# Adding the products of a GpSimd convolution in two instructions of 256 columns instead of one of 512

## The chip, the cores and the metric

The kernel runs on one core of a Trainium2 chip. The metric is the device time of one execution in microseconds (us). TensorE multiplies matrices, VectorE, ScalarE and GpSimd work elementwise, and SyncE issues the transfers from memory; in rows of the profile they are PE (PEld for its weight loads), DVE, ACT, POOL and SP.

## What is computed

Two transformer blocks on 512 tokens of 1024 channels. The change is in the first layer of the second block, layer A, whose mixer is this:

```python
def conformer_conv(u, conv_w, conv_b, g, b):
    a, gl = jnp.split(u, 2, axis=-1)
    h = a * jax.nn.sigmoid(gl)
    h = jnp.pad(h, ((0, 0), (CONV_KERNEL - 1, 0), (0, 0)))
    h = lax.conv_general_dilated(h, conv_w[:, None, :].astype(h.dtype), (1,), 'VALID',
                                 dimension_numbers=('NWC', 'WIO', 'NWC'),
                                 feature_group_count=CONV_WIDTH_2) + conv_b
    return jax.nn.silu(layer_norm(h, g, b))
```

That is a convolution along the tokens, channel by channel, with 31 taps on 1536 channels, and then a layer norm over the channels. Beside it the layer computes attention to a memory of 256 rows, a gate, and an output projection.

## The kernel before

Activations lie with channels on the 128 partitions and the 512 tokens along the columns, so 1536 channels are 12 tiles of 128x512. Matrix products are exact to float32 by splitting: each weight tile is loaded to `raw`, ScalarE copies it to `whi` (the high part) and VectorE computes `wlo` = `raw` - `whi` (the low part, `prep`, L445 to L455), and TensorE makes three products of the parts (`mm3`, L457). A product can't start before its `wlo` is there. I call the instruction at L453 a split. There are 3 buffers for `raw`, and 4 each for `whi` and `wlo`.

`conv_tile(j)` (L1134 to L1162) makes one of the 12 tiles of the convolution. Two projections give the gate and the value; VectorE writes their product to `pad`, which has 30 leading columns set to 0 by GpSimd. The 31 taps are shared out over the engines (`NOFF, NPE = 11, 1`, L591):
- tap 0: ScalarE writes the sum `cg`.
- taps 1 to 10: ScalarE multiplies a shifted view of `pad` by the tap's weight into `tm`, and GpSimd adds `tm` to `cg` in one instruction of 128x512 (L1149 to L1152). That is 10 adds to a tile and 120 in all.
- tap 11: TensorE, by a diagonal matrix, into a PSUM bank `cp`.
- taps 12 to 30: VectorE adds them to `cp`, 19 instructions to a tile (L1160), 228 in all. They read one operand from SBUF and one from PSUM.

VectorE then adds `cp` to `cg` (L1161), and the layer norm `lnc` (L1132, class `LN`) takes the tile: GpSimd subtracts a mean from it and adds up its squares. Gate tiles, attention and part of the output projection are woven between the 12 tiles (`weave`, L1011 and L1203).

No engine runs in this order of the text. The class `Program` records every instruction (L137), and `order` (L233) makes a plan from estimated durations: at each moment every free engine takes the ready instruction with the best priority. `emit` (L359) repeats that 12 times with new priorities, keeps the plan with the earliest end, and issues the instructions in its order. Each engine then runs its own list strictly in that order. Three properties of the plan matter here:
- It follows dependencies by whole tiles (L148 to L156), so two writes to different columns of one tile depend on each other. Between dependent GpSimd instructions it puts 102 ns (L52).
- It treats instructions marked `port` as exclusive, over VectorE and GpSimd together. Every GpSimd instruction over more than 8 columns is marked (L188), and on VectorE those with two wide operands from SBUF, such as the split (L186). VectorE's taps are not.
- A marked instruction whose port is taken at the moment when its engine is free is passed over, and the engine takes the next ready one:

```python
                    if o.port and port > now:
                        heapq.heappush(events, port)
                        continue
```

It charges a GpSimd instruction with two operands `n * 2.2 + 99` ns for n columns (L188).

Of the kernel before, what the change touches and what calls it, by code (L numbers as in the profile page):

```python
# [13 lines left out]
ALU = mybir.AluOpType  # L14
# [4 lines left out]
T = 512  # L19
# [11 lines left out]
SSD = 600  # L31
# [16 lines left out]

# [1 line left out]
ENGINES = ("PE", "ACT", "DVE", "POOL", "SP")  # L50
# [8 lines left out]
class View:  # L59
    """a lazily resolved access pattern of a tile"""  # L60

# [60 lines left out]
class Program:  # L122
    """records instructions in program order, then orders each engine's by a list schedule"""

# [71 lines left out]
    def latest(s, prio):  # L196
        """latest starts, from a list schedule of the reversed program"""
        ops = s.ops
        need = [len(o.succ) for o in ops]
        when = [0.0] * len(ops)  # L200
        ready = {e: [] for e in ENGINES}
        wait = [(0.0, -prio[o.idx], o.idx) for o in ops if not o.succ]
        heapq.heapify(wait)
        busy = dict.fromkeys(ENGINES, 0.0)
        events, port = [0.0], 0.0
        while events:
            now = heapq.heappop(events)
            while wait and wait[0][0] <= now:
                _, p, k = heapq.heappop(wait)
                heapq.heappush(ready[ops[k].eng], (p, k))  # L210
            for e, q in ready.items():
                if busy[e] > now or not q:
                    continue
                o = ops[q[0][1]]
# [3 lines that stand above are left out]
                heapq.heappop(q)  # L218
                end = now + (o.dur + 1500 if e == "SP" else o.dur)
                busy[e] = now + o.dur  # L220
                if o.port:
                    port = end
                heapq.heappush(events, busy[e])
                when[o.idx] = -end
                for d in o.deps:
                    when[d] = max(when[d], end + s.latency(ops[d], o))
                    need[d] -= 1
                    if need[d] == 0:
                        heapq.heappush(wait, (when[d], -prio[d], d))
                        heapq.heappush(events, when[d])  # L230
        return when

    def order(s, prio, window):  # L233
# [3 lines left out]
        left, first, last = {}, {}, {}  # L237
        for o in ops:
            for x in o.tiles:
                left[x] = left.get(x, 0) + 1  # L240
                first.setdefault(x, o.idx)
                last[x] = o.idx
        # slots in use if the rest ran in program order: a tile may take one early only if this never exceeds the number there is
        live = {g: np.zeros(len(ops) + 1, np.int32) for g in free}
# [7 lines left out]
        early, wait, back = [], [], deque()  # L252
# [9 lines left out]
        while len(seq) < len(ops):  # L262
# [5 lines left out]
            while fin and fin[0][0] <= now:  # L268
                o = ops[heapq.heappop(fin)[1]]
# [10 lines left out]
            while back and back[0][0] <= now:  # L280
                x = back.popleft()[1]
# [10 lines left out]
            for e, q in ready.items():  # L292
# [3 lines left out]
                while q:  # L296
                    p, k = heapq.heappop(q)
                    o = ops[k]
# [23 lines left out]
                o = ops[best[1]]  # L322
# [58 lines left out]
def body(ctx, tc, t, out):  # L381
# [10 lines left out]
    V, S, G, TE = DVE, ACT, POOL, PE  # L392
# [26 lines left out]

# [1 line left out]
    mhalf = const("mhalf", (P, 1))  # L421
# [21 lines left out]

# [1 line left out]
    def prep(src, kt, w=P):  # L445
# [47 lines left out]

# [1 line left out]
    def tok_sum(tiles, n=T):  # L495
# [27 lines left out]
    class LN:  # L523
        """layer norm over tiles that come one by one, centred first by the mean of the first npil tiles, whose sum is then 0"""

# [28 lines left out]
        def finish(s):  # L554
            """broadcast rows r, q with norm = centred * r - q"""
            ps = bank("C")
            for o, x in ((0, s.s1.acc), (4, s.s2.acc)):
                for b in range(4):
                    TE.matmul(ps[:, o + b:o + b + 1], x[:, b * P:(b + 1) * P], ones[:, 0:1],
                              start=o + b == 0, stop=o + b == 7, skip_group_check=True)  # L560
            mv = small([P, 8], "mv")
            V.tensor_scalar(mv, ps[:, 0:8], 1.0 / s.dim, None, op0=ALU.mult)
            v = small([P, 4], "rv")
            V.tensor_tensor(v, mv[:, 0:4], mv[:, 0:4], op=ALU.mult)
            V.scalar_tensor_tensor(v, mv[:, 4:8], LN_EPS, v, op0=ALU.add, op1=ALU.subtract)
            r = rpow(v)
            q = small([P, 4], "rq")
            V.tensor_tensor(q, mv[:, 0:4], r, op=ALU.mult)
            return tok_bcast(r), tok_bcast(q, tag="B")
# [21 lines left out]
    NOFF, NPE = 11, 1  # L591
    # ================= block 1, mixer =================
    def load_x():
# [25 lines left out]

    # time steps of all heads  # L620
    raw = act()[:, :P]
# [28 lines left out]
    V.tensor_tensor(v3(dtr), v3(dtr), dtb.rearrange("p (o k) -> p o k", o=1).to_broadcast([P, 4, 16]), op=ALU.add)  # L650
    # softplus(x) = max(x, 0) + log1p(exp(-|x|)), log1p(e) = 2 atanh(e / (2 + e))
    ex, den, s2, po = s64(), s64(), s64(), s64()
# [18 lines left out]
    acs, cdec, dec = den, s2, s64()  # L671
    # cumulated steps as rows of heads
    ps = bank("B")[0:16, :]
# [14 lines left out]

    # causal convolution of xs, B, C; order of the channel tiles: B0 B1 C0 C1, then xs
    conv = {}  # L690
# [13 lines left out]

    # z gate
    zs = []
# [5 lines left out]

    # B in token rows, B C products
    triu_b = triu.rearrange("p (o k) -> p o k", o=1).to_broadcast([P, 4, P])
# [83 lines left out]

    # multi-scale pool
    icnt = const("icnt", (P, 64))  # L800
# [56 lines left out]

    # keys and values of the first memory
    def load_mem(src):
# [74 lines left out]

    # normalised SSD branch
    yhl = [split_g(conv[j], vc("ssd_norm", j)) for j in range(8)]
# [10 lines left out]

    # ================= block 1, cross attention =================
    def cols(x, b):
        return [a[:, b * P:(b + 1) * P] for a in x]  # L950

    class XAttn:
        """two heads (2 pr, 2 pr + 1) of 4; q: nd tiles [dims, T] per head; scale(tb): a number or a column per token"""

# [56 lines left out]
    def weave(*lists):  # L1011
        """emits the lists of steps in turns, each spread evenly over the longest"""
        n = max(len(x) for x in lists)
        pos = [0] * len(lists)
        for i in range(n):
            for k, x in enumerate(lists):
                want = -(-(i + 1) * len(x) // n)
                while pos[k] < want:
                    x[pos[k]]()
                    pos[k] += 1  # L1020
# [9 lines left out]
    q = []  # L1030
# [13 lines left out]
    xs = [XAttn(pr, q, kT, vN, 2, lambda tb: qs[:, tb:tb + 1], emit1) for pr in range(2)]  # L1044
# [8 lines left out]

    # ================= block 1, swiglu =================
    rB = tok_bcast(rsq(tok_sum([ss.acc]), D, EPS))
# [23 lines left out]

    # taps of layer A: sigmoid(x) = (1 + tanh(x / 2)) / 2, and the half goes to the taps; some as diagonal matrices  # L1080
    cwh = vec2[:, 0:372]
# [38 lines left out]

    # ================= final norm of block 1 =================
    rB = tok_bcast(rsq(tok_sum([ss.acc]), D, EPS))
    x, u = [], []
# [5 lines left out]
    MS = 128.0 ** -0.5  # L1129
    # ================= block 2, layer A =================  # L1130
    K0 = NOFF + NPE if NPE else NOFF + 1
    lnc = LN(1536, 8, G)  # L1132

    def conv_tile(j):  # L1134
# [14 lines left out]
        for k in range(1, NOFF):  # L1149
            tm = act(tag="tm")  # L1150
            S.activation(tm, tap(k)[0], AF.Copy, scale=tap(k)[1])
            G.tensor_tensor(cg, cg, tm, op=ALU.add)  # L1152
        cp = bank("B")
# [17 lines left out]
    def gate_tile(w, j, half=False):  # L1171
        """silu(gate); with half, twice that from tanh"""
        ps = dense(wrange(w, j, 8), u)
        gate[j] = act()
        if half:
            th = act(tag="th")
            S.activation(th, ps, AF.Tanh, scale=0.5)
            V.scalar_tensor_tensor(gate[j], th, 1.0, ps, op0=ALU.add, op1=ALU.mult)
        else:
            S.activation(gate[j], ps, AF.Silu)  # L1180
# [6 lines left out]
    def out_tile(w, j, part, first, ln=None):  # L1187
        """part: the operands by row tile"""
        ks = sorted(part)
        ps = dense(wrange(w, j, len(ks), ks[0]), [yhl[k] for k in ks])  # L1190
        if first:
            V.scalar_tensor_tensor(x[j], x[j], ALPHA, ps, op0=ALU.mult, op1=ALU.add)
        else:
            V.tensor_tensor(x[j], x[j], ps, op=ALU.add)
        if ln:
            ln.add(x[j])
# [28 lines left out]

    # ================= block 2, layer B =================
    NQ0 = 6
# [101 lines left out]

    # token rows for the last layer norm  # L1330
    yN = [[act(), act()] for _ in range(4)]
# [48 lines left out]

    # last projection, token rows
    grow, brow = [act(), act()], [act(), act()]
# [151 lines left out]
```

## Time and profile before

| | |
|---|---|
| median of 3 runs | 1707.15 us (1706.2 to 1710.0) |
| span of the profiled execution, first to last instruction | 1705.8 us |
| its mean granted TensorE clock | 0.992 |
| busy: PE, DVE, ACT, POOL | 98%, 67%, 45%, 25% |

One execution was profiled. What lies around its span isn't printed apart; the median of the runs is 1.35 us above the span.

How to read the rows: nearly every instruction bears line L378, where the plan is issued, so groups are told apart by tiles: `B<-pad,vec,B` is a tap on VectorE, `wlo<-raw,whi` a split, and `act<-act,act` on POOL an addition. A row of a timeline has start, length, engine, line, operation, tiles, shapes and count, and in brackets the idle time before it with its releaser; lengths hold all instructions of the row. A row by form has count, then busy us and mean ns of one, then the idle time before. A row of a stretch has its bounds and length, then busy us (and count) of PE, PEld, DVE, ACT and POOL, the granted clock of TensorE (1.00 is full), and the share and rate of the transfers.

### The profile page before, as it was taken

How to read it: one execution, taken by the hardware profiler on the slowest of the kernel's cores; microseconds unless marked ns; L12 is line 12 of the kernel's file. 1: busy time of each engine (PE TensorE's matmuls, PEld its weight loads, DVE VectorE, ACT ScalarE, POOL GpSimd, SP SyncE). 2: the span in 40 equal slices, each digit the busy share in tenths (PEclk: the TensorE clock that was granted, in tenths of full speed). 3: DMA queues.
4: the chain of work that ended last, by engine and by line, in shares of the span. 5: the costliest groups of instructions: out<-in, count | busy, mean ns of one | idle time of the engine just before them, and what ended most of it. 6: DMA issues, size and time to landing. Idle time of an engine off the chain costs nothing. (4 is left out here: it accounts for less than half of the span.)

```text
span 1705.8 us, 21241 instructions
## 1 busy us (share of the span) xinstructions
PE 1665.2 (98%) x7966; PEld 1361.4 (80%) x7966; DVE 1142.2 (67%) x1801; ACT 775.9 (45%) x1349; POOL 421.0 (25%) x325
## 2 busy tenths in 40 slices
PE   9999999999999999999999997999899999999998
PEld 7888678888888888888878775778787788788886
DVE  7836778574565435544477999988747895467754
ACT  6722444444553222332356766545435434545541
POOL 1004433020031001201233678965630000000000
PEclk9999999999999999999999998999999999999999
DMA  7321212531242333322323311232233123211121
GB/s 242 117 86 56 93 50 87 160 99 50 75 131 93 98 99 99 95 79 90 117 91 108 102 56 50 81 127 87 75 124 115 62 99 94 80 63 50 53 84 50
DMA packets 49719, 156.32 MB, mean 92 GB/s; under 512 B 5648, under 2 KB 7568, under 8 KB 49616
## 3 DMA queue, kind: packets, MB, share of 16 engines
q1 hardware_dynamic: 49616, 154.96, 28.2%
q8 instruction: 63, 1.03, 0.3%
q14 instruction: 40, 0.33, 0.1%
HBM read 152.71 MB, written 2.10 MB: 91 GB/s over the span
## 5 line engine op out<-in xcount | busy, mean ns | idle before, releaser
L378 PE MATMUL mm<-act,whi 128*128 128x512 f32 (+1 forms) x3888 | 1194.3, 388 | 18.5 <-DVE act L378 12.9
L378 PEld LDWEIGHTS mm<-act,whi 128*128 128x128 f32 x3888 | 717.8, 189 | 174.3 <-ACT act L378 15.3
L378 PE MATMUL mm<-act,wlo 128*128 128x512 f32 (+1 forms) x1944 | 749.4, 388 | 9.8 <-DVE wlo L378 9.6
L378 ACT ACTIVATE whi<-raw 128x1024 fp32r<-128x1024 f32 (+3 forms) x293 | 289.4, 991 | 582.0 <-PE mm L378 352.5
L378 POOL TENSOR_TENSOR act<-act,act 128x512 f32<-128x512 f32 (+1 forms) x252 | 372.5, 1493 | 683.7 <-DVE act L378 314.8
L378 DVE TENSOR_TENSOR wlo<-raw,whi 128x1024 fp32r<-128x1024 f32 (+3 forms) x293 | 373.2, 1281 | 123.7 <-ACT whi L378 118.9
L378 PEld LDWEIGHTS mm<-act,wlo 128*128 128x128 f32 x1944 | 366.9, 189 | 85.5 <-DVE wlo L378 11.3
L378 DVE TENSOR_TENSOR act<-mm,act 128x512 f32<-128x512 f32 (+3 forms) x173 | 114.6, 664 | 244.9 <-PE mm L378 236.9
L378 ACT ACTIVATE act<-act 128x512 f32<-128x512 f32 (+2 forms) x222 | 134.7, 617 | 104.6 <-DVE act L378 65.9
L378 DVE SCALAR_TENSOR_TENSOR B<-pad,vec,B 128x512 f32<-128x512 f32 x228 | 167.2, 753 | 5.7 <-PE B L378 1.5
L378 DVE TENSOR_TENSOR act<-act,act 128x512 f32<-128x512 f32 (+3 forms) x203 | 138.3, 711 | 26.2 <-ACT act L378 25.3
L378 POOL TENSOR_TENSOR fr<-fv,mhalf 128x1 f32<-128x1 f32 x4 | 2.2, 547 | 410.5 <-DVE fv L378 410.5
L378 ACT ACTIVATE act<-pad,vec 128x512 f32<-128x512 f32 x144 | 94.8, 730 | 11.6 <-DVE pad L378 11.4
L378 PE MATMUL A<-act,act 128*128 128x256 f32 (+6 forms) x488 | 97.8, 342 | 0.3
L378 PEld LDWEIGHTS A<-act,act 128*128 128x128 f32 (+1 forms) x488 | 72.1, 189 | 16.7 <-issue 5.6
L378 PE MATMUL mm<-whi,act 128*128 128x512 f32 x264 | 85.0, 393 | 0.0
L378 ACT ACTIVATE act<-C 128x128 f32<-128x128 f32 (+4 forms) x164 | 52.2, 359 | 70.6 <-PE C L378 68.3
L378 PE MATMUL B<-act,act 128*128 128x128 f32 (+2 forms) x492 | 71.0, 284 | 0.0
L378 PEld LDWEIGHTS B<-act,act 128*128 128x128 f32 (+1 forms) x492 | 61.7, 167 | 9.6 <-issue 3.4
L378 ACT ACTIVATE act<-mm 128x512 f32<-128x512 f32 (+3 forms) x92 | 51.7, 566 | 18.4 <-PE mm L378 18.3
L378 PEld LDWEIGHTS mm<-whi,act 128*128 128x128 f32 x264 | 49.4, 188 | 9.6
L378 PE MATMUL mm<-wlo,act 128*128 128x512 f32 x132 | 51.8, 393 | 0.0
(130 smaller groups left out, 965.6 us busy)
## 6 DMA issues: line engine op xcount, KB each, us to landing
raw<-in_w_g_dram SPq DMA_DIRECT2D x22, 512.0 KB, 3.3
raw<-in_w_u_dram SPq DMA_DIRECT2D x22, 512.0 KB, 3.3
raw<-in_w_om_dram SPq DMA_DIRECT2D x16, 512.0 KB, 3.8
raw<-in_w_d_dram SPq DMA_DIRECT2D x16, 512.0 KB, 3.5
raw<-in_a_gate_dram SPq DMA_DIRECT2D x16, 512.0 KB, 3.4
raw<-in_b_gate_dram SPq DMA_DIRECT2D x16, 512.0 KB, 3.3
raw<-in_b_wo_dram SPq DMA_DIRECT2D x16, 512.0 KB, 3.3
raw<-in_w_xbc_dram SPq DMA_DIRECT2D x12, 512.0 KB, 4.2
```

Source lines behind the costliest of these rows:

```text
L378: r = o.fn(*[real(a) for a in o.args], **{k: real(v) for k, v in o.kw.items()})
```

## The change

Each of the 120 additions becomes two, one on columns 0 to 255 and one on columns 256 to 511. Apart from this only comments and docstrings are taken out.

```diff
         for k in range(1, NOFF):
             tm = act(tag="tm")
             S.activation(tm, tap(k)[0], AF.Copy, scale=tap(k)[1])
-            G.tensor_tensor(cg, cg, tm, op=ALU.add)
+            for o in (0, T // 2):
+                G.tensor_tensor(cg[:, o:o + T // 2], cg[:, o:o + T // 2], tm[:, o:o + T // 2], op=ALU.add)
         cp = bank("B")
```

## Rows read from the trace of the kernel before

**Rows 1.** Part 1 of the page: busy us, share of the span, instructions.

```profile
PE 1665.2 (98%) x7966; PEld 1361.4 (80%) x7966; DVE 1142.2 (67%) x1801; ACT 775.9 (45%) x1349; POOL 421.0 (25%) x325
```

**Rows 2.** Busy time by stretch, around the convolution: PE, PEld, DVE, ACT, POOL.

```profile
860.00:960.00 100.00, 96.61 (x459) 78.38 (x458) 84.91 (x118) 65.21 (x122) 43.55 (x33) 1.00 0.29 92
960.00:1060.00 100.00, 90.53 (x381) 69.47 (x380) 96.99 (x139) 62.61 (x119) 77.21 (x61) 0.95 0.20 66
1060.00:1120.00 60.00, 55.61 (x234) 42.98 (x233) 58.33 (x71) 34.53 (x51) 51.04 (x36) 1.00 0.29 92
1120.00:1180.00 60.00, 60.00 (x268) 49.09 (x266) 50.02 (x57) 31.11 (x45) 42.55 (x30) 1.00 0.35 115
```

**Rows 3.** Waits of PE from 1020 to 1060: us in total, times, longest.

```profile
PE mm L378 <- DVE wlo L378: 9.2, 1, 9.2
```

**Rows 4.** Busy time by stretch, around that wait.

```profile
1040.00:1050.00 10.00, 2.32 (x6) 1.83 (x7) 10.00 (x15) 2.79 (x6) 9.92 (x7) 0.56 0.07 24
1052.00:1060.00 8.00, 8.00 (x37) 6.62 (x36) 7.87 (x14) 2.76 (x5) 5.45 (x4) 1.00 0.40 136
```

**Rows 5.** Timeline of DVE from 1019 to 1050.

```profile
1019.36 1.27 DVE L378 TENSOR_TENSOR wlo<-raw,whi 128x1024 fp32r<-128x1024 f32 x1
...
1031.22 0.68 DVE L378 TENSOR_TENSOR act<-act,B 128x512 f32<-128x512 f32 x1
...
1034.54 11.96 DVE L378 SCALAR_TENSOR_TENSOR B<-pad,vec,B 128x512 f32<-128x512 f32 x18
1046.41 2.96 DVE L378 TENSOR_TENSOR wlo<-raw,whi 128x1024 fp32r<-128x1024 f32 x3
```

**Rows 6.** Timeline of ACT from 1019 to 1032: the high parts for those splits.

```profile
1019.49 1.07 ACT L378 ACTIVATE whi<-raw 128x1024 fp32r<-128x1024 f32 x1 [2.39 <-PE mm L378]
...
1027.44 1.05 ACT L378 ACTIVATE whi<-raw 128x1024 fp32r<-128x1024 f32 x1
...
1030.87 0.64 ACT L378 ACTIVATE whi<-raw 128x512 fp32r<-128x512 f32 x1 [0.55 <-ACT act L378]
```

**Rows 7.** Timeline of POOL from 1011 to 1050.

```profile
1011.65 19.41 POOL L378 TENSOR_TENSOR act<-act,act 128x512 f32<-128x512 f32 x14
...
1035.29 15.22 POOL L378 TENSOR_TENSOR act<-act,act 128x512 f32<-128x512 f32 x10 [0.38 <-ACT act L378]
```

**Rows 8.** Groups of POOL by form, from 882 to 892.5 and from 243 to 251.

```profile
L378 POOL TENSOR_TENSOR act<-act,act 128x512 f32<-128x512 f32 x8 | 10.3, 1293 | 24.2 <-ACT act L378 23.6
...
L378 POOL TENSOR_TENSOR act<-act,act 128x384 f32<-128x384 f32 x4 | 4.0, 1009 | 8.6 <-ACT act L378 8.6
```

**Rows 9.** Timeline of POOL from 882 to 892.5: one tile's additions, each after its own predecessor.

```profile
882.45 10.89 POOL L378 TENSOR_TENSOR act<-act,act 128x512 f32<-128x512 f32 x8 [23.63 <-ACT act L378]
```

**Rows 10.** Timeline of POOL from 981.9 to 989.6.

```profile
980.73 10.05 POOL L378 TENSOR_TENSOR act<-act,act 128x512 f32<-128x512 f32 x8
```

**Rows 11.** Groups of DVE by form from 880 to 1180.

```profile
L378 DVE TENSOR_TENSOR wlo<-raw,whi 128x1024 fp32r<-128x1024 f32 x45 | 63.7, 1436 | 4.9 <-ACT whi L378 4.7
L378 DVE TENSOR_TENSOR wlo<-raw,whi 128x512 fp32r<-128x512 f32 x8 | 9.9, 1273 | 0.0
...
L378 DVE TENSOR_SCALAR xm<-xm 128x2 f32<-128x2 f32 x8 | 3.5, 445 | 0.0
```

**Rows 12.** Two tiles on DVE, 880 to 1180: ns of one, min/median/max; first, last start.

```profile
L378 DVE TENSOR_TENSOR wlo<-raw,whi x53: 685/1225/2316, 881.1 to 1179.5; 128x1024 fp32r<-128x1024 f32 x45, 128x512 fp32r<-128x512 f32 x8
...
L378 DVE TENSOR_SCALAR xm<-xm x8: 159/183/1234, 907.2 to 997.2; 128x2 f32<-128x2 f32 x8
```

**Rows 13.** Groups by form in the collision from 1081 to 1092: DVE, then POOL.

```profile
L378 DVE TENSOR_TENSOR wlo<-raw,whi 128x512 fp32r<-128x512 f32 x5 | 7.9, 1622 | 0.0
...
L378 POOL TENSOR_TENSOR act<-act,act 128x512 f32<-128x512 f32 x5 | 8.1, 1648 | 0.0
```

**Rows 14.** Waits of PE from 1060 to 1120.

```profile
PE mm L378 <- DVE act L378: 2.3, 2, 1.5
```

**Rows 15.** Additions on POOL from 1046 to 1051: ns of one, min/median/max.

```profile
L378 POOL TENSOR_TENSOR act<-act,act x3: 1283/1290/4024, 1045.1 to 1050.6; 128x512 f32<-128x512 f32 x3
```

## The prediction

> **What bounds the kernel now.** I read the busy shares first: TensorE is busy for 1665.2 of 1705.8 us [rows 1], so only 40.6 us of the span can come off without taking work from TensorE, and an edit on GpSimd, busy for 25%, counts only where TensorE waits for what it delays or frees. So the next view is the stretches around the convolution [rows 2]. From 860 to 960 TensorE misses 3.4 us. From 960 to 1060 it misses 9.5 us while VectorE is busy for 96.99 of 100 us, and from 1060 to 1120 it misses 4.4 us while VectorE is busy for 58.33 of 60. From 1120 to 1180 it misses nothing. The reader is to see that VectorE sets the pace between 960 and 1120, and GpSimd, with 77 and 51 us, is near it.
>
> The waits of TensorE name what is late: one wait of 9.2 us for a split [rows 3]. The clock then shows a second price: the granted clock is 0.56 of full speed from 1040 to 1050, so partly at the lower level of 1.2 GHz behind the idle stretch, and 1.00 again from 1052 [rows 4]. The wait ends with the first of three splits, which start at 1046.41 and take 2.96 us together [rows 5], so at about 1047.6; some 4 us of work then ran at half speed, a loss of about 2 us. This one place costs about 11 us.
>
> Why was the split late? Its inputs were not: the high parts were ready by 1020.6, 1028.5 and 1031.5 [rows 6]. VectorE instead ran taps, 18 of them from 1034.54 [rows 5]. GpSimd added nearly without a pause from 1011.65 to 1050 [rows 7]. That is the plan's doing: a split needs the port, a tap on VectorE doesn't, and whenever VectorE was free in the plan an addition held the port, so the split was passed over until the run of additions thinned out. So the long additions act twice: in the plan they push splits back, and on the chip they hold VectorE up when the two meet.
>
> **The change, step by step.**
>
> GpSimd's own time. An addition of 512 columns takes 1.293 us, one of 384 takes 1.009 [rows 8], so 2.22 ns a column, and 256 columns come to 0.725 us by that line, an estimate. What counts is the spacing. Eight additions to one sum take 10.89 us, (10.89 - 1.29) / 7 = 1.371 us apart [rows 9]; eight later ones, with work on other sums between, take 10.05 us, 1.251 apart [rows 10]. Waiting for the predecessor's result thus costs 0.12 us. A half is 256 x 2.22 = 0.568 us less, 0.683 apart, and two halves make 1.366 us a tap. Each half's predecessor lies one instruction back, so the 0.12 us is hidden. Against 1.371 that is nothing, against 1.251 it is 0.115 more: 120 taps make between 0 and 13.8 us of GpSimd, and I take the middle, 7 us. The bounds are wider: pieces that cost half of the whole would save the 0.12 us, -14 us, and pieces as dear as 384 columns (0.97 apart, 1.94 a tap) add 0.57 to 0.69, up to 83 us; I take the line because 256 is as near to 384 as that is to 512. Cover: GpSimd is idle 56 of 100, 23 of 100, 9 of 60 and 17 of 60 us in the four stretches [rows 2], 105 us together, so on TensorE's path this costs 0. If the cover goes, VectorE's sum of both parts is late, and behind it wait the next splits and taps: the addition run ended at 1031.06 [rows 7], and VectorE took that sum at 1031.22 [rows 5], 0.16 us later. Some 30 taps fall in the tightest stretch, and 30 x 0.115 = 3.5 us is the price there. Issuing 120 more instructions has no row of its own; the spacings above contain it.
>
> VectorE's waits for the port. A split of 1024 columns has a median of 1.225 us and a mean of 1.436, one of 512 takes 0.685 at best and 1.273 in the mean; the two-column instruction of the attention 0.159 at best and 0.445 in the mean [rows 11, 12]. The excess is 45 x 0.211 + 8 x 0.588 + 8 x 0.286 = 9.5 + 4.7 + 2.3 = 16.5 us. An addition under way is waited out, so halves should cut it in half, 8 us of VectorE. TensorE sees what falls where VectorE sets the pace. That is the collision from 1081 to 1092, where five splits took 1.622 us each [rows 13], 4.7 us of excess; half is 2.3. TensorE's waits for VectorE in that stretch total 2.3 us [rows 14], and its missing time 4.4, so I take -2 us, between 0 and -4.
>
> The Trainium skill (SBUF — State Buffer, "SBUF: two separate sides") says that the shared port is an exclusive lock, held for a whole instruction by whoever starts first. The 1.622 us of a split that takes 0.685 alone agree [rows 12, 13]. By that rule an addition would lose one VectorE instruction at most, but one of 4.02 us, beside three splits of 2.96 us together, stood through all of them [rows 5, 15]; the rule alone would give -2 us here, and the row adds the risk of the third rival below.
>
> The plan. The plan changes as a whole, since 120 instructions, their durations and their priorities do, and no row can show the new order. For the split at 1046 the bounds are the whole stall back, -11 us, and a stall half again as long, +6. With one tile's additions in flight, the plan leaves the port free for 102 ns behind each half, twice as often as now, so a passed-over split finds it sooner; with two tiles in turns there is no such gap. I take -4 us, a bit over a third of the stall, since the run before 1046 is of both kinds: its first 14 additions are (19.41 - 1.29) / 13 = 1.39 us apart, like one tile's, and the nine from 1035.29, without the one of 4.02, are 15.22 - 4.02 = 11.2 us, 1.24 apart [rows 7].
>
> Sum: 0 - 2 - 4 = -6 us. The profiled execution's span is 1705.8, the sum gives 1699.8; the median of the runs lies 1.35 above that span, so 1701 us.
>
> **The rivals.**
>
> Nothing reaches TensorE. The splits meet shorter additions, but the stalls stand where the plan puts them, and the saved 8 us are slack on VectorE. For it: the stretch with the 9.2 us stall holds hardly any port waiting (the split before it took 1.27 us, the three at its end 2.96 [rows 5], against a median of 1.225 for the long form [rows 12]). Time 1704 to 1710, say 1706.
>
> The port is taken for longer (the other side). The plan charges two halves 8% more than a whole, and a hundred ns behind each half for the whole-tile dependency. If runs of additions are fed by two tiles, the port is never free between, and the runs are 8% longer: of the 36 us from 1011 to 1047 that is 3 us more for the split behind, and the same for the run of GpSimd around 1081 [rows 2]; each microsecond of stall brings a part of it again at the low clock. 3 + 3 us and 2 of the clock make +8: 1715 us. It decides if additions of two tiles alternate through the stretch, as the spacing of 1.24 us says for part of it; against it, a second tile's additions need not overlap when each plan is drawn anew.
>
> VectorE splits the taps. Between two halves VectorE can take the port where a whole addition would have gone through. In the collision an addition took 1.648 us instead of 1.293 [rows 13], 0.355 more; the 16.5 us of excess, at half an addition or 0.6 us a meeting, make some 28 meetings, and a second one for each tap that has one costs 28 x 0.355 = 10 us of GpSimd; I put under half of it behind the 0.16 us of slack, +4 us: 1711 us.
>
> **How the numbers follow.** Forecast 0.42, nothing reaches TensorE 0.25, port taken for longer 0.23, taps split 0.10. A measurement of this kernel tells about 0.2% from no change, 3.4 us. The forecast's own range is 1692 (the whole 11 us and 4 us of waits) to 1703. Over all cases 1692 to 1718: the upper end is the second rival with the stall half again as long. Faster by over 0.2% has 0.42, within 0.25, slower 0.23 + 0.10 = 0.33.
>
> **What would show it.** Right: the additions of 256 at about 0.73 us, spaced 0.68; splits of 1024 in the convolution with a mean near 1.33 instead of 1.436; TensorE's longest wait for a split under 9 us, and a granted clock of 1.00 around it. The no-effect case shows the first two and the same stall. The second rival shows splits bunched behind longer runs of additions and more missing TensorE time from 960 to 1120; the third shows VectorE waiting for GpSimd before it sums the two parts. The prediction is wrong if the plan moves stalls to a place that has none now, such as the stretch after 1120, or if a half takes 1 us or more.

## The result: slower by 43 us

The changed kernel takes 1749.56 us (median of 4 runs, 1746.69 to 1753.19) against 1706.77 us (4 runs) of the kernel before on the same chip: a ratio of 1.0243, interval 1.0225 to 1.0262. The forecast was 1701, and the range ended at 1718.

The profiled execution of the changed kernel has a span of 1747.6 us and a granted clock of 0.981. Part 1 of its page, the row that answers to [rows 1]:

```profile
PE 1678.9 (96%) x7966; PEld 1369.8 (78%) x7966; DVE 1165.5 (67%) x1801; ACT 774.8 (44%) x1349; POOL 421.3 (24%) x445
```

GpSimd has 120 instructions more and is busy for the same time, 421.3 against 421.0 us. TensorE is idle for 1747.6 - 1678.9 = 68.7 us, where it was 40.6: 28.1 more. The same 7966 matmuls keep it busy for 13.7 us more, which fits the lower granted clock in the rows below; it isn't timed apart. The two make 41.8 us, the difference of the spans. The stretches of [rows 2] say where; the columns are the same:

```profile
860.00:960.00 100.00, 96.83 (x453) 78.33 (x452) 82.23 (x113) 63.62 (x110) 46.98 (x59) 1.00 0.30 98
960.00:1060.00 100.00, 83.60 (x343) 64.30 (x342) 91.34 (x115) 57.59 (x117) 65.96 (x94) 0.88 0.15 50
1060.00:1120.00 60.00, 46.98 (x168) 33.41 (x167) 58.78 (x74) 28.92 (x50) 49.46 (x53) 0.89 0.18 56
1120.00:1180.00 60.00, 53.19 (x229) 42.48 (x228) 55.45 (x62) 32.36 (x47) 56.47 (x69) 0.96 0.28 92
```

The first stretch is as before. In the other three TensorE misses 16.4, 13.0 and 6.8 us (9.5, 4.4 and 0 before), and the granted clock falls to 0.88, 0.89 and 0.96. VectorE is busy for 91.34 us from 960 to 1060 and finishes fewer instructions in it, 115 against 139. So its instructions have become longer. The groups of VectorE by form from 880 to 1180, which answer to [rows 11]:

```profile
L378 DVE TENSOR_TENSOR wlo<-raw,whi 128x1024 fp32r<-128x1024 f32 x36 | 59.5, 1663 | 13.6 <-ACT whi L378 13.3
L378 DVE TENSOR_SCALAR xm<-xm 128x2 f32<-128x2 f32 x8 | 15.5, 1946 | 0.0
L378 DVE TENSOR_TENSOR wlo<-raw,whi 128x512 fp32r<-128x512 f32 x8 | 8.0, 997 | 0.0
```

An instruction on two columns, which the plan doesn't mark `port` because it is so narrow, takes 1.946 us in the mean. The tiles' views, with minimum, median and maximum (880 to 1190; compare [rows 12]), show that one or two of each group do it:

```profile
L378 DVE TENSOR_SCALAR xm<-xm x8: 157/169/7499, 905.4 to 1023.6; 128x2 f32<-128x2 f32 x8
...
L378 DVE TENSOR_TENSOR wlo<-raw,whi x47: 678/1226/10022, 881.3 to 1190.0; 128x1024 fp32r<-128x1024 f32 x39, 128x512 fp32r<-128x512 f32 x8
```

The medians are those of before. The maxima are 7.5 and 10.0 us, where those of [rows 12] went to 2.316. The timeline of VectorE around the first of them, and that of GpSimd beside it:

```profile
970.38 0.75 DVE L378 SCALAR_TENSOR_TENSOR B<-pad,vec,B 128x512 f32<-128x512 f32 x1
971.04 7.50 DVE L378 TENSOR_SCALAR xm<-xm 128x2 f32<-128x2 f32 x1
978.45 0.68 DVE L378 SCALAR_TENSOR_TENSOR act<-act,mm 128x512 f32<-128x512 f32 x1
```

```profile
970.43 8.08 POOL L378 TENSOR_TENSOR act<-act,act 128x256 f32<-128x256 f32 x11
```

The row of GpSimd is one run of additions without a pause, from 970.43 to 978.51, and VectorE's instruction ends at 978.54. It was shut out of the port for 7.34 us: through the half that was under way, an addition of the layer norm and nine more halves, all eleven of that row. The form of the halves in this stretch (972 to 977):

```profile
L378 POOL TENSOR_TENSOR act<-act,act 128x256 f32<-128x256 f32 x7 | 4.8, 730 | 0.0
```

Each takes 0.730 us, and those from 972.34 to 977.78 start 0.680 us apart: the next one has started before the one ahead of it has ended. I call such a run **closed**. TensorE's longest wait in 965 to 980 is what the shut-out costs it:

```profile
PE mm L378 <- DVE act L378: 5.3, 1, 5.3
```

There are three such waits. The second is the same instruction at 1023.61, 6.94 us long, behind a run of GpSimd from 1021.72 to 1030.53. The third is a split, here on the timeline of VectorE from 1168 to 1186, beside the run of GpSimd from 1160 to 1186:

```profile
1171.72 10.02 DVE L378 TENSOR_TENSOR wlo<-raw,whi 128x1024 fp32r<-128x1024 f32 x1
```

```profile
1158.81 21.86 POOL L378 TENSOR_TENSOR act<-act,act 128x512 f32<-128x512 f32 x30
```

Beyond their lengths alone the three waits make 7.34 + 6.78 + 8.80 = 22.9 us. They are not all of it: the waits of TensorE from 860 to 1260 are

```profile
PE mm L378 <- DVE act L378: 22.9, 9, 7.8
PE mm L378 <- DVE wlo L378: 18.3, 3, 8.6
PE mm L378 <- ACT act L378: 5.9, 3, 3.7
```

and 5.3 + 7.8 + 8.6 = 21.7 of these 47.1 us stand behind the three. The rest stands at places where VectorE waited for nothing unusual, but got its work late. The change thus did two things, and the experiments part them: it drew another plan, and it cut the additions.

### The profile page after: what moved, and what is told of

Read it like the earlier page. It is cut to its first block, busy times and chain, and to the rows that moved or that the text cites. A ratio compares the mean times of both kernels' runs of the same rounds, so it can differ in the third digit from the quotient of the medians.

```text
span 1747.6 us, 21365 instructions
## 1 busy us (share of the span) xinstructions
PE 1678.9 (96%) x7966; PEld 1369.8 (78%) x7966; DVE 1165.5 (67%) x1801; ACT 774.8 (44%) x1349; POOL 421.3 (24%) x445
## 4 chain that ended last, share of the span: by engine, by line
PE 85%; DVE 10%; ACT 2%; issue 2%; POOL 0%; DMA 0%; SPq 0%; DVEq 0%; POOLq 0%; ACTq 0%
PE mm L378 74%; PE A L378 5%; PE B L378 4%; DVE B L378 4%; DVE act L378 3%; PE C L378 3%; ACT act L378 2%; DVE wlo L378 1%; DVE xm L378 1%; ACT whi L378 1%; POOL act L378 0%; DMA act<-in_xT_dram 0%; DVE pad L378 0%; POOL rn L378 0%; SPq L378 0%
## 5 line engine op out<-in xcount | busy, mean ns | idle before, releaser
L378 PE MATMUL mm<-act,whi 128*128 128x512 f32 (+1 forms) x3888 | 1198.8, 390 | 34.0 <-DVE act L378 25.2
L378 PEld LDWEIGHTS mm<-act,whi 128*128 128x128 f32 x3888 | 722.5, 190 | 193.9 <-DVE act L378 25.4
L378 PE MATMUL mm<-act,wlo 128*128 128x512 f32 (+1 forms) x1944 | 749.6, 389 | 18.4 <-DVE wlo L378 18.3
L378 ACT ACTIVATE whi<-raw 128x1024 fp32r<-128x1024 f32 (+3 forms) x293 | 289.1, 989 | 594.5 <-PE mm L378 366.3
L378 POOL TENSOR_TENSOR act<-act,act 128x256 f32<-128x256 f32 (+2 forms) x372 | 372.0, 1034 | 705.0 <-DVE act L378 339.5
L378 DVE TENSOR_TENSOR wlo<-raw,whi 128x1024 fp32r<-128x1024 f32 (+3 forms) x293 | 377.1, 1291 | 144.1 <-ACT whi L378 139.0
L378 PEld LDWEIGHTS mm<-act,wlo 128*128 128x128 f32 x1944 | 369.6, 190 | 94.7 <-DVE wlo L378 20.1
L378 DVE TENSOR_TENSOR act<-mm,act 128x512 f32<-128x512 f32 (+3 forms) x173 | 114.6, 663 | 243.6 <-PE mm L378 235.8
L378 ACT ACTIVATE act<-act 128x512 f32<-128x512 f32 (+2 forms) x222 | 133.7, 615 | 114.8 <-DVE act L378 75.1
L378 DVE SCALAR_TENSOR_TENSOR B<-pad,vec,B 128x512 f32<-128x512 f32 x228 | 164.3, 750 | 4.3 <-PE B L378 1.3
L378 DVE TENSOR_TENSOR act<-act,act 128x512 f32<-128x512 f32 (+3 forms) x203 | 146.4, 749 | 30.9 <-ACT act L378 28.7
L378 POOL TENSOR_TENSOR fr<-fv,mhalf 128x1 f32<-128x1 f32 x4 | 2.2, 548 | 410.5 <-DVE fv L378 410.5
L378 PE MATMUL A<-act,act 128*128 128x256 f32 (+6 forms) x488 | 100.2, 346 | 0.9 <-ACT act L378 0.9
L378 ACT ACTIVATE act<-pad,vec 128x512 f32<-128x512 f32 x144 | 94.2, 727 | 7.8 <-DVE pad L378 7.8
L378 PEld LDWEIGHTS A<-act,act 128*128 128x128 f32 (+1 forms) x488 | 73.1, 191 | 17.8 <-ACT act L378 6.2
L378 PE MATMUL mm<-whi,act 128*128 128x512 f32 x264 | 84.6, 392 | 0.0
L378 ACT ACTIVATE act<-C 128x128 f32<-128x128 f32 (+4 forms) x164 | 51.8, 360 | 67.4 <-PE C L378 65.0
L378 PE MATMUL B<-act,act 128*128 128x128 f32 (+2 forms) x492 | 71.8, 290 | 0.0
L378 PEld LDWEIGHTS B<-act,act 128*128 128x128 f32 (+1 forms) x492 | 62.5, 170 | 9.3 <-issue 4.5
L378 ACT ACTIVATE act<-mm 128x512 fp32r<-128x512 f32 (+3 forms) x92 | 51.6, 565 | 14.5 <-PE mm L378 14.4
L378 PEld LDWEIGHTS mm<-whi,act 128*128 128x128 f32 x264 | 49.4, 188 | 9.7
L378 ACT ACTIVATE act<-act,vec 128x512 fp32r<-128x512 f32 (+3 forms) x68 | 46.4, 700 | 21.4 <-DVE act L378 18.0
(130 smaller groups left out, 981.9 us busy)
```

Of the source, the lines that this page charges most:

```text
L378: r = o.fn(*[real(a) for a in o.args], **{k: real(v) for k, v in o.kw.items()})
```

## The experiments

All ran with timed rounds against the kernel before on the same chip; a difference in us is that of the medians. A **long wait** is an instruction of VectorE that took 3 us or more beyond its length alone, between 870 and 1190. The kernel before has none.

### The plan and the cut apart

**The cut alone.** One recorded addition, planned and charged as before, issues two halves; every engine's order is that of before.

```diff
-            G.tensor_tensor(cg, cg, tm, op=ALU.add)
+            prog.rec("POOL", add_halves((0, T // 2)), "tensor_tensor", (cg, cg, tm), dict(op=ALU.add))
```

> The order of the kernel before on every engine, but each addition is issued as two halves at its place (the plan sees one addition, as before). Theory A (the port: halves of one tile follow one another without the gap that a wait for the predecessor leaves, and VectorE gets in only at such a gap): some VectorE instructions wait 3 us or more for the end of a run of halves, and the time is 1717 to 1740 us. Theory B (the plan: the new order is bad, the chip treats halves as it treats wholes): within 4 us of before, 1703 to 1711, and no VectorE instruction waits over 1.3 us beyond its own length. My first account (shorter pieces, shorter waits): 1700 to 1706.

Measured: 1733.52 us, +26.0, ratio 1.0154 (1.0138 to 1.0171). The tiles of VectorE (880 to 1190), and the waits of TensorE (860 to 1260):

```profile
L378 DVE TENSOR_TENSOR wlo<-raw,whi x48: 678/1220/7390, 879.8 to 1186.4; 128x1024 fp32r<-128x1024 f32 x40, 128x512 fp32r<-128x512 f32 x8
L378 DVE TENSOR_SCALAR xm<-xm x8: 160/176/4148, 909.5 to 1003.6; 128x2 f32<-128x2 f32 x8
```

```profile
PE mm L378 <- DVE wlo L378: 25.1, 5, 14.0
PE mm L378 <- DVE act L378: 11.1, 5, 5.9
```

Six long waits, of 3.2 to 6.2 us, 29.4 us together. So the cut costs 26 us with no change of the order at all, as theory A has it.

**The plan alone.** The changed kernel's order, with nothing issued at the place of the first half and the whole addition at the place of the second.

```diff
             for o in (0, T // 2):
-                G.tensor_tensor(cg[:, o:o + T // 2], cg[:, o:o + T // 2], tm[:, o:o + T // 2], op=ALU.add)
+                prog.rec("POOL", add_whole(cg, tm) if o else nothing, "tensor_tensor",
+                         (cg[:, o:o + T // 2], cg[:, o:o + T // 2], tm[:, o:o + T // 2]), dict(op=ALU.add))
```

> The order of the changed kernel on every engine, but one whole addition stands at the place of each second half, and nothing at the place of the first. Theory A: the three waits of 6.9, 7.5 and 10 us on VectorE are gone, and some 23 us of the 43 with them, plus a part for the low clock: 1712 to 1726. Theory B: 1742 to 1756, with the stalls where the changed kernel has them.

Measured: 1735.29 us, +27.8, ratio 1.0160 (1.0145 to 1.0175). So the order costs 28 us with whole additions too. The time lies between the two expectations: theory A missed the order's own price, theory B that of the cut. One long wait of 7.65 us is in it, a split at 1157.49, here on the timelines of VectorE and of GpSimd:

```profile
1157.49 8.87 DVE L378 TENSOR_TENSOR wlo<-raw,whi 128x1024 fp32r<-128x1024 f32 x1
```

```profile
1146.63 13.78 POOL L1138 TENSOR_TENSOR act<-act,act 128x512 f32<-128x512 f32 x11
1160.36 1.27 POOL L378 TENSOR_TENSOR act<-act,act 128x512 f32<-128x512 f32 x1
1161.58 3.71 POOL L1138 TENSOR_TENSOR act<-act,act 128x512 f32<-128x512 f32 x3
```

L1138 is the convolution's addition, L378 one of the layer norm. Each begins before the one ahead has ended, the eleven of the convolution 1.25 us apart, the spacing of additions to different sums [rows 10], and the split ends at 1166.36. A closed run can thus be made of whole additions as well, when successive ones belong to different sums.

**The halves turned.** In every second tap the second half goes first, so that at each border between two taps a half follows another of the same columns and has to wait for it. In the changed kernel:

```diff
-            for o in (0, T // 2):
+            for o in ((0, T // 2) if k % 2 else (T // 2, 0)):
```

> The changed kernel, with the order of the two halves turned round in every second tap, so that one pair in two touches the same half twice and waits for its predecessor. The order of everything else and the number of instructions are those of the changed kernel. Theory A: a gap once per tap lets VectorE in, no wait over 1.5 us beyond an instruction's own length, 1712 to 1728. Theory B: no different from the changed kernel, 1745 to 1753. If the gap matters only together with the length of the pieces, it lies between.

Measured: 1737.0 us, +29.5, ratio 1.0173 (1.0156 to 1.0190); two long waits, 6.3 and 6.8 us, 13.1 us together. The splits (880 to 1190):

```profile
L378 DVE TENSOR_TENSOR wlo<-raw,whi x49: 677/1225/8021, 881.6 to 1189.5; 128x1024 fp32r<-128x1024 f32 x41, 128x512 fp32r<-128x512 f32 x8
```

Theories A and B both miss; the time lies between them. The first of the two waits stands beside five whole additions and one half, where turning the halves makes no gap. And the same with the order of before, `add_halves((0, T // 2) if k % 2 else (T // 2, 0))`:

> The order of the kernel before, halves issued at the place of each addition, turned round in every second tap as in the run before this one. Theory A: a gap once per tap as in the kernel before, so 1702 to 1712, at least 10 us under the same order with halves not turned round. Theory B: the same as that run and as the kernel before.

Measured: 1710.39 us, +2.9, ratio 1.0018 (1.0009 to 1.0028). One long wait is left, of 3.1 us; the tile of the splits (880 to 1190):

```profile
L378 DVE TENSOR_TENSOR wlo<-raw,whi x53: 673/1301/4365, 883.2 to 1184.3; 128x1024 fp32r<-128x1024 f32 x45, 128x512 fp32r<-128x512 f32 x8
```

The count and the size of the halves are those of the first kernel above, and 23 of its 26 us are gone. It is the sequence that costs, not the number of halves.

### The gap

**Whole additions without a gap.** The order of before; in every second tap GpSimd doubles `tm` in place instead of adding it, so those taps are missing in the sum, and no addition follows its own predecessor.

> The order of the kernel before on every engine, with whole instructions of 512 columns. In every second tap the addition to the sum is replaced by one that doubles the tap's product in its own tile, so the sum lacks these taps and hardly any addition waits for its predecessor. Theory A (the missing gap shuts VectorE out, whatever the size of the pieces): waits of 3 us or more on VectorE as with halves, 1715 to 1740 us, though GpSimd does nothing in smaller pieces. Theory S (small pieces shut VectorE out): no VectorE wait over 1.3 us beyond its own length, 1702 to 1710.

Measured: 1708.01 us, +0.8, ratio 1.0004 (0.9995 to 1.0014). The forms of GpSimd (860 to 1260; L1135 is the doubling), and the splits (880 to 1190):

```profile
L1135 POOL TENSOR_TENSOR act<-act 128x512 f32<-128x512 f32 x60 | 69.2, 1159 | 0.0
```

```profile
L378 DVE TENSOR_TENSOR wlo<-raw,whi x53: 678/1220/2349, 880.8 to 1179.6; 128x1024 fp32r<-128x1024 f32 x45, 128x512 fp32r<-128x512 f32 x8
```

No long wait, though the runs are closed. That is what theory S (small pieces) expected, and theory A missed: a closed run doesn't always shut VectorE out. A weakness: a doubling reads one tile, not two, and is shorter than an addition.

**Halves that share a column.** The order of before, 240 pieces, but of 257 columns each for the first (0 to 256) and 256 for the second (256 to 511). Every piece then has to wait for the piece of its own sum ahead of it.

```diff
+    def add_overlapping(a, b, c, op):
+        for lo, hi in ((0, T // 2 + 1), (T // 2, T)):
+            nc.gpsimd.tensor_tensor(a[:, lo:hi], b[:, lo:hi], c[:, lo:hi], op=op)
```

> The order of the kernel before, each addition issued as two pieces of 257 columns that share column 256, so every piece has to wait for the piece right before it (column 256 gets each tap twice; that is the one wrong column). Theory gap (VectorE is shut out only by pieces that follow each other without waiting): every piece ends before the next starts, spacing about 0.80 us instead of 0.68, GpSimd busier by some 30 us, and still no wait of VectorE of 3 us or more; time between 1700 and 1715 us, against 1733.5 with separate halves in the same order. Rival, number of pieces (240 instructions are more meetings than 120, gap or not): waits of 3 us and more stay, and the time stays at 1728 to 1740. Rival, GpSimd too slow: no long waits, but sums come late and the time is over 1720 with waits of TensorE for VectorE's sum of both parts.

Measured: 1712.14 us, +4.4, ratio 1.0027 (1.0018 to 1.0037). Part 1, the tiles of VectorE (880 to 1190), the forms of GpSimd, and the waits of TensorE (860 to 1260):

```profile
PE 1667.4 (98%) x7966; PEld 1363.0 (80%) x7966; DVE 1142.9 (67%) x1801; ACT 774.8 (45%) x1349; POOL 459.0 (27%) x445
```

```profile
L378 DVE TENSOR_TENSOR wlo<-raw,whi x53: 685/1306/2307, 879.6 to 1181.8; 128x1024 fp32r<-128x1024 f32 x45, 128x512 fp32r<-128x512 f32 x8
L378 DVE TENSOR_SCALAR xm<-xm x8: 157/168/621, 905.7 to 993.6; 128x2 f32<-128x2 f32 x8
```

```profile
L1136 POOL TENSOR_TENSOR act<-act,act 128x257 f32<-128x257 f32 x120 | 105.7, 881 | 58.8 <-ACT act L378 54.1
L1136 POOL TENSOR_TENSOR act<-act,act 128x256 f32<-128x256 f32 x120 | 103.8, 865 | 9.4
```

```profile
PE mm L378 <- DVE wlo L378: 9.3, 1, 9.3
```

GpSimd is busy for 32 us longer than with separate halves (427.1 there), pieces start 0.82 us apart in the median instead of 0.70, and from 870 to 1190 every second piece of a tap starts 0.08 us after the end of the first. Of the first pieces right behind a second one 65 of 92 do so too; the other 27 start before its end, as pieces of another sum can. Yet the kernel is 21.4 us faster: all six long waits are gone, and the longest of the two-column instructions takes 0.621 us. The wait of 9.3 us is that of [rows 3] again, which goes with the order. So it is not the number of the pieces that shuts VectorE out; pieces of the same number and nearly the same size, with gaps between most of them, don't.

**The same in the changed kernel.** Its own order and its 240 pieces, the first of each tap one column longer.

```diff
-                G.tensor_tensor(cg[:, o:o + T // 2], cg[:, o:o + T // 2], tm[:, o:o + T // 2], op=ALU.add)
+                prog.rec("POOL", add_one_more(cg, tm) if o == 0 else nc.gpsimd.tensor_tensor, "tensor_tensor",
+                         (cg[:, o:o + T // 2], cg[:, o:o + T // 2], tm[:, o:o + T // 2]), dict(op=ALU.add))
```

> The changed kernel with its own order and its 240 pieces, but the first piece of each tap has 257 columns, so that it shares column 256 with the second (which gets each tap twice; that is the one wrong column) and the two have to wait for each other. Theory gap: the waits of VectorE of 6.8, 7.3 and 8.8 us in the changed kernel go, with at most one of 3 us or more left where pieces of two tiles alternate; GpSimd is busier by about 30 us; time 1725 to 1737, against 1749.6 for the changed kernel, which leaves what the order alone costs (whole additions in this order: 1735.3 with one wait of 7.6 us, so about 1728 without it). Rival, the order alone sets the time and the waits do not reach TensorE: 1743 to 1755 whatever the waits do.

Measured: 1733.22 us, +26.8, ratio 1.0151 (1.0130 to 1.0173), so 16.3 us less than the changed kernel. The splits (880 to 1190):

```profile
L378 DVE TENSOR_TENSOR wlo<-raw,whi x50: 683/1225/8010, 881.5 to 1186.3; 128x1024 fp32r<-128x1024 f32 x42, 128x512 fp32r<-128x512 f32 x8
```

One long wait of 6.8 us is left, a split from 1157.30 to 1165.31. It stands in a run where the pieces of two sums take turns, so that none follows its own predecessor, and it ends at the run's first gap, from 1164.23 to 1164.31, here on the timeline of GpSimd from 1150 to 1166:

```profile
1163.51 0.72 POOL L378 TENSOR_TENSOR act<-act,act 128x256 f32<-128x256 f32 x1
1164.31 1.59 POOL L1137 TENSOR_TENSOR act<-act,act 128x257 f32<-128x257 f32 x1
```

The long waits fell from 22.9 to 6.8 us, by 16.1; the time by 16.3.

### What the plan is worth

The plan was then redrawn with whole additions, by nothing but the number that it charges for one (1225 ns in the kernel before): `prog.ops[-1].dur += 1` and the like behind the addition.

> The kernel before with whole additions; only the plan's charge for each of the 120 additions is 1 ns longer, and every order is drawn anew. Theory C (the plan is a draw: any small difference gives another order, and the one of the kernel before is a good draw): 1712 to 1740 us, about as far off as the changed kernel's order with whole additions, which was 28 us slower. Theory D (what the halves are charged makes the plan bad: two fixed parts and a 102 ns gap to each tap): within 4 us of before, 1703 to 1711.

> The same with a charge 10 ns longer, a second draw. Theory C: again anywhere from 1712 to 1740, and not the time of the run with 1 ns. Theory D: 1703 to 1712.

> The same with a charge 201 ns longer, which is what two halves and one gap of 102 ns are charged together (1426 for 1225 ns), still in one piece. Theory D: 1725 to 1745, nearer to the changed order than to before, while 1 and 10 ns stay at before. Theory C: 1712 to 1740, no worse than with 1 and 10 ns.

> Whole additions, charged 202 ns longer instead of 201. Theory C: some other time, over 5 us away from the 1733.8 us of 201 ns as likely as not, from 1710 to 1740. Theory D': 1728 to 1740, beside its neighbour.

> Whole additions, charged 1 ns less than in the kernel before. Theory C: from 1708 to 1740. Theory D': 1704 to 1716, beside the kernel before and the run with 1 ns more.

> Whole additions as before; the plan charges each 100 ns less (1125 instead of 1225 ns). Theory draw (any redrawn plan is worse than the one in the kernel before by a random 5 to 25 us): 1712 to 1732, like a charge of 1 or 10 ns more. Rival, length (a longer charge keeps the port taken for longer in the plan and pushes splits back, so a shorter one frees it): 1700 to 1710. The chip runs them longer than planned, which both ignore.

> Whole additions as before, charged 200 ns less. Theory draw: 1712 to 1732, no order by length (not better than at -100). Rival, length: not above the time at -100, and below 1710.

> Whole additions as before, charged 200 ns more, the third kernel around that length (201 ns more gave 1733.8, 202 gave 1728.8). Rival, length: again 1727 to 1736, so three of three stand 20 us and more above the kernel before, where charges within 10 ns stood 5 to 14 above. Theory draw: anywhere from 1710 to 1735; under 1722 it would show that length has no hold on the time.

And two kernels of another kind: two pieces in the plan whose charges with the 102 ns between them come to those of one whole addition (whole additions are issued), and a plan that doesn't mark the additions as `port`.

> The plan sees two pieces to a tap, as in the changed kernel, but charges them with the 102 ns between them exactly what it charges one whole; one whole addition is issued at the second piece's place. Theory C (a draw): 1710 to 1735. Theory D' (a longer charge makes the plan worse, in one piece or two): 1706 to 1720, under the 1734 us of the charge longer by 201 ns.

> The kernel before, but the plan no longer marks the 120 additions as taking the port, so it doesn't pass over the splits of the weights while additions run. My first account of the 9.2 us stall (the plan pushes splits behind additions): no wait of TensorE for a split over 4 us in the convolution; the splits then meet additions on the chip more often, over 40 times instead of 23. Time by that account 1695 to 1706 if what it gains isn't lost to those meetings; theory A (a split that meets a run without gaps waits for its end): single waits of 3 us or more on VectorE, 1715 to 1745.

| plan | time, us | over before | ratio |
|---|---|---|---|
| charge -200 ns | 1722.89 | +15.1 | 1.0090 (1.0075 to 1.0105) |
| -100 ns | 1726.10 | +18.3 | 1.0105 (1.0088 to 1.0122) |
| -1 ns | 1713.68 | +6.4 | 1.0037 (1.0024 to 1.0050) |
| +1 ns | 1712.16 | +6.0 | 1.0032 (1.0017 to 1.0047) |
| +10 ns | 1719.86 | +13.7 | 1.0080 (1.0058 to 1.0102) |
| +200 ns | 1722.65 | +14.9 | 1.0087 (1.0072 to 1.0102) |
| +201 ns | 1733.81 | +27.7 | 1.0163 (1.0147 to 1.0178) |
| +202 ns | 1728.79 | +21.6 | 1.0119 (1.0104 to 1.0134) |
| two pieces, same charge | 1719.93 | +12.7 | 1.0068 (1.0053 to 1.0084) |
| additions not `port` | 1725.77 | +19.6 | 1.0110 (1.0093 to 1.0127) |
| halves' plan, whole additions (above) | 1735.29 | +27.8 | 1.0160 (1.0145 to 1.0175) |

None of the first ten has a long wait. A single nanosecond of charge redraws the plan and costs 6 us; between +200 and +201 lie some 13 us (27.7 - 14.9). Charges of 100 and 200 ns less lose as much as 200 more does. So the length of the charge alone does not set the time; which plan is drawn does, and each of eleven new ones was worse than the old one. A part of length isn't excluded: the two longest charges, +201 and +202, are the worst two, as theories D and D' said, and +200, at 1722.65, came in below the 1727 to 1736 of the length theory but not under the 1722 that would have ruled length out. How the old plan came to be better than eleven others is open; with twelve plans drawn alike, a given one would be the best in one case of twelve. The stalls stand elsewhere each time. With +10 ns the longest wait of TensorE (860 to 1260) is one for GpSimd:

```profile
PE C L378 <- POOL act L378: 16.6, 1, 16.6
```

With -100 ns it is work of VectorE that isn't a split:

```profile
PE mm L378 <- DVE act L378: 22.3, 8, 9.3
```

The plan without `port` on the additions tests the account of the 9.2 us stall [rows 3]. Its waits for splits from 860 to 1260:

```profile
PE mm L378 <- DVE wlo L378: 4.1, 5, 1.2
```

None is longer than 1.2 us, as that account expected, but this doesn't show it: with the rule in force the redraws by +10 ns and by two pieces have none over 1.1 us either, and -200 ns none over 1.4. The other expectations missed: the time, the long waits of theory A, and the meetings (26 splits from 870 to 1190 took over 0.1 us more than alone, 19 in the kernel before, not over 40). The kernel is slower, by stalls at other places.

No kernel here beats the one before.

## Why the prediction was wrong

Its sign was wrong, and two steps failed: the lost gap between GpSimd's instructions, which the sum put at 0, and the redrawn plan, which it put at -4 us. By the runs the 43 us are about 27 us of plan (27.8 with whole additions in the new order, 26.8 with pieces that share a column, each with one long wait of its own in it) and 15 to 16 us that go with the long waits only the halves have (42.8 over before, against 27.8 and 26.8). The two parts depend on each other: in the old order the same cut costs 26 us. The table sets long waits beside times, order by order:

| kernel | long waits, us | over before, us |
|---|---|---|
| old order: whole; doubled; sharing a column | 0; 0; 0 | 0; +0.8; +4.4 |
| old order: halves turned | 3.1 | +2.9 |
| old order: halves | 29.4 | +26.0 |
| new order: sharing a column | 6.8 | +26.8 |
| new order: whole | 7.6 | +27.8 |
| new order: halves turned | 13.1 | +29.5 |
| new order: halves (the change) | 22.9 | +42.8 |

- **GpSimd's own time: right.** Halves of 0.73 us, 0.68 us apart, were forecast; 0.730 and 0.680 were measured. GpSimd's busy time rose by 0.3 us, and by 6.1 in the old order (427.1 against 421.0), inside the 0 to 13.8 us; both hold waits for the port.
- **"Each half's predecessor lies one instruction back, so the 0.12 us is hidden", and a cost of 0: wrong, and the first of the two failures.** The spacing was right and its meaning was missed. The 0.12 us in [rows 9] were read as a loss of GpSimd; they were also where VectorE got the port. With the gap brought back (pieces that share a column, old order) GpSimd is 32 us busier and the kernel 21 us faster.
- **"Halves should cut it in half, 8 us of VectorE" (-2 us): wrong, and the term in which the first failure shows.** The excess from 880 to 1180, worked out as in the prediction, is 36 x 0.438 + 8 x 0.312 + 8 x 1.787 = 32.6 us instead of 16.5. Without the three long waits 9.7 are left, near the forecast 8, but partly because fewer long splits fall into the window (36 for 45): an instruction loses 9.7 / 52 = 0.19 us instead of 16.5 / 61 = 0.27, a third less and not half. What failed is the premise that a waiting instruction waits out one addition. At 971.04 it waited out eleven. The Trainium skill (SBUF — State Buffer, "SBUF: two separate sides") says that whoever starts first gets the pair of ports for the whole instruction; the trace agrees that the other is blocked, and shows that the end of the instruction need not be its turn. The addition of 4.02 us beside three splits [rows 15], in the prediction only a risk to GpSimd, was the same thing the other way round: the second and the third of those splits start 0.09 us before the one ahead has ended.
- **The plan (-4 us, bounds -11 to +6): wrong, the second failure, and the larger.** The bounds came from the one stall that the old plan has. But a new plan sets every stall of the convolution anew, and the old one bounds only what can be won back, not what can be lost. Measured: +28, and +6 to +28 over all redraws.
- **The rivals.** "Nothing reaches TensorE" failed: TensorE is idle for 28.1 us more. "The port is taken for longer" had the sign, at 1715 us. Its mechanism, a longer charge, isn't borne out as the main one: charges of 100 and 200 ns less lose 18 and 15 us. "VectorE splits the taps" can't be the price of 43 us: 38 us more of GpSimd than before (459.0 against 421.0), in the kernel whose pieces share a column, come with +4.4 us, about the +4 that this rival gave.
- **What would make it wrong** was named: stalls at a place that has none now. From 1120 to 1180, where TensorE missed nothing [rows 2], it misses 6.8 us.
- **The account of the old stall** (the plan passes a split over while an addition holds the port) fits the plan without `port` and is not shown by it, since other redraws lose that stall too. The stall itself goes with the order: it is back, at 9.2 and 9.3 us, with doublings and with pieces that share a column.

## What to carry to other kernels

Where two engines share a port, a short pause between the instructions of one let the other in here every time, and a run without pauses could shut it out to its end: before cutting or reordering them, look in the timeline for rows without a gap, and then at the maximum, not the mean, of the other engine's instructions. Where a planner draws the order from estimated costs, an edit of one instruction is a new draw of the whole kernel: test the edit with the old order held, and price the draw by a few plans with charges off by a nanosecond. Bounds for a redrawn plan come from such redraws, not from the stall that one hopes to remove.

## What the runs showed of the hardware

Three things were not expected.

- An instruction of VectorE that needs the shared port can be shut out through a whole run of GpSimd's instructions. One of two columns, 0.16 us alone, took 7.50 us beside eleven additions, the longest split 10.02 us where 1.22 is its length alone. All 14 long waits lasted until GpSimd's run ended (eleven of them) or until the first gap in it (three).
- All 14 stand in closed runs, in which an addition starts some 0.045 us before the one ahead has ended. A wait for the predecessor turns that into a gap of 0.08 us (medians of the kernels with separate halves and with a shared column, in the old order), and the six long waits with it into none.
- A closed run is not sufficient. Whole additions and doublings in the old order stand in closed runs too and made no long wait; whole additions in the new order did it once, for 7.65 us, and a closed run of halves can let a split in after one of them. All nineteen traces were counted from 870 to 1190, each split and two-column instruction at the first end of a GpSimd instruction for which it had waited 0.045 us or more while another followed. At a gap VectorE got in 206 times of 206. In closed runs it was passed over 15 times of 249: 11 of 63 between two pieces of 256 or 257 columns, 3 of 31 between a piece and a whole, 1 of 155 between two wholes. So small pieces are passed over more often, but only where the gap is missing. What decides at one such place stays open; so does how much of the halves' plan's 28 us is more than the luck of the draw, since the ten other draws reach from 6 to 27.7.
